# A two-layer flow-matching block: the latents' first stages written between the context's selection and its rows, and two raised priorities taken away

## The chip, the cores and the metric

The kernel runs on one core of one Trainium2 chip. The metric is the device time of one execution in microseconds (us), the median of several runs. Engines are named as in the profile: PE (matrix products, PEld its weight loads), DVE (vector engine), ACT (activations), POOL (GpSimd, which here also issues the indirect fetches), SP (issues the other transfers).

## What is computed

Two streams of 256 tokens of width 1024 go through two layers: the latents `x` and a context `z`. A layer is a mixer (a gated delta-rule scan in two directions, a pooling and a Fourier part, one output product) and a retrieval from 16384 experts, each with a residual. The latents' scan starts from the context's final scan state. The context is not updated in the second layer.

```python
def _peer(h, w_query, sub_keys, expert_u, expert_v):
    q = (h @ w_query).reshape(t, PEER_HEADS, 2, PEER_KEY_HALF)
    scores = jnp.einsum('thpc,hpnc->thpn', q, sub_keys)
    s_top, i_top = lax.top_k(scores, PEER_TOPK)            # 16 of 128, per head and half
    cand = s_top[:, :, 0, :, None] + s_top[:, :, 1, None, :]
    best, pos = lax.top_k(cand.reshape(t, PEER_HEADS, -1), PEER_TOPK)
    idx = ...                                              # 8 heads x 16 experts per token
    gate = jax.nn.softmax(best, axis=-1)
    act = gelu(einsum('td,thkd->thk', h, expert_u[idx]))
    return einsum('thk,thkd->td', gate * act, expert_v[idx])
```

## The kernel before

**Stages of layer 0 in the order of time.** The context's mixer runs first (`columns`, `scan`, `update`). Then two pieces of work are open side by side, and the change is about their order:

- The **context's retrieval**. `gather_select` scores the keys head by head (the products `po<-hT,w`, weights `in_wq` through one buffer per half, then `s<-keys,q` on L801) and picks the best on DVE (`select`, L772 to L884, with the multiply `oh` on POOL). Its last act is a transpose of the indices through PSUM bank `c2` (`c<-ident,idx_f`, L949, copied to `idx_t` on L950). Then `gather_rows` fetches one expert row per token and choice with indirect transfers from POOL (L970). For the first 128 tokens (`by_choice`) these are 128 fetches of `u` (512 KB each, seven buffers) with a dot product on DVE (L982) for each, and then 128 fetches of `v` with small products on PE (L1005) into PSUM bank `s`. For the other 128 tokens (`by_token`) there are 128 fetches of `uv`, 1 MB each. The loop `for _ in range(EARLY)` draws the first 256 fetches, all of `by_choice`, here; the rest is drawn in the middle of the stream below.
- The **latents' first stages**. `columns` makes the projections (`pj<-hT,w`, `pj<-w,hT`, the convolutions on L495 and L497) and the scan's gates (from L428 on, through the same single bank `c2`), `scan` makes the chunked scan (the multiplies `C<-L,levels`, `qd`, `kb`, `vb`, `kf` and the state's `S<-S,dc` run on POOL), `update` the output product and residual (L743 to L761), `dense_select` the latents' own selection, and `build` writes a table of gates (`gs`, L1089, L1090).

Then `stream` runs over all 128 blocks of experts for the latents (`first` L1118 to L1120, `second` L1141); its first product needs bank `s`, which `by_choice` holds until its last sum (L1010). The last 128 fetches run beside it, and after them the context's part of layer 1. Layer 1 then repeats mixer, selection and stream for the latents.

**What sets the order.** When the kernel is built, each engine gets one fixed list of instructions. The builder takes, among the instructions that are ready by its own estimate of time, the one with the highest priority. Priority is the place in the program, unless a block raises it: `tc.high_priority(AHEAD)` with `AHEAD = 100000` puts its block ahead of all that is written before it. Buffers and PSUM banks are given out in the order of the program. On the chip each engine works through its list in that order and stops where an operand is late.

Of the kernel before, what the change touches and what calls it, by code (L numbers as in the profile page):

```python
# [24 lines left out]
CTX, LAT = 0, 1  # L25
# [120 lines left out]
def _body(st, tc, a, out, dbg, until):  # L146
# [16 lines left out]
    def nm(s):  # L163
        n_names[0] += 1
        return f"{s}_{n_names[0]}"
# [46 lines left out]
    def dump(key, t):  # L212
        if dbg is not None and key in dbg:
            nc.sync.dma_start(dbg[key], t)
# [16 lines left out]
    def pool_tt(out, x, y, op):  # L231
        pool.tensor_tensor(out, x, y, op=op)  # L232
# [165 lines left out]
    def heads(tag, f):  # L398
        p = bank([128, 4, 128], tag)
        for h in range(4):  # L400
            f(p[:, h], h)
        return p
# [330 lines left out]
    def update(l, s, m, state, po, tl):  # L733
        zs, mix = state["zs"], state["mix"]
        parts = (("dmixh", F32R), ("dmixl", F32R)) if roles["split"] else (("dmix", F32),)
        dmix = [tl(name, [128, 4, T], 1, dt) for name, dt in parts]

        for b in range(NB):
            ot = tl(f"ot{b}", [128, 4, 128])
            ss = tl(f"ssq{b}", [128, 4])  # L740
            for h in range(4):
                act.activation(ot[:, h], po[b][:, h], AF.Square, accum_out=ss[:, h : h + 1])
            dve.tensor_scalar(ss, ss, 1.0 / 128, EPS, op0=OP.mult, op1=OP.add)  # L743
            r = rsqrt(ss, 4, f"c{b}")
            dve.tensor_tensor(ot, po[b], r[:, :, None].to_broadcast([128, 4, 128]), OP.mult)
            dve.tensor_tensor(ot, ot, zs[:, b].rearrange("p (h n) -> p h n", h=4), OP.mult)
            p = heads(f"c{b}", lambda o, h: pe.transpose(o, ot[:, h], ident))
            o = slice(b * 128, b * 128 + 128)
            if roles["split"]:
                act.copy(dmix[0][:, :, o], p)  # L750
                dve.tensor_tensor(dmix[1][:, :, o], p, dmix[0][:, :, o].bitcast(F32), OP.subtract)
            else:
                act.copy(dmix[0][:, :, o], p)
        dump(f"mixa{l}{s}", dmix[0])
        for n in range(2):
            g1 = in_rows(m[:, 2, :, s], n, "row1")
            cs = slice(n * 512, n * 512 + 512)
            for b, p in enumerate(columns_by_token(f"wout{l}", n, lambda k: [x[:, k % 4] for x in (dmix, mix)[k // 4]])):
                t = tl("upd", [128, 512], 2)
                dve.tensor_tensor(t, p, g1, OP.mult)  # L760
                dve.tensor_tensor(X[s, b][:, cs], X[s, b][:, cs], t, OP.add)  # L761
        for b in range(NB):
            dump(f"xm{l}{s}{b}", X[s, b])
# [278 lines left out]
    TG, IG = 16, 8  # L1042
    LAG = (17, 32)
    ROWS, EARLY = 7, 256
    AHEAD = 100000
    HB = {"u": 2, "v": 2}

    def dense_select(l, s, m, dp, side):

        Hh = dp("Hh", [128, KT, T], 1, F32R)  # L1050
        Hl = dp("Hl", [128, KT, T], 1, F32R)
        sp = Stage("select", side)
        chosen = dp("chosen", [128, 3, T])
        sc, sh = scales(l, 1, m, s)
        xns = [normed(X[s, b], sp("xn", [128, D], 2), f"n{b}") for b in range(NB)]
        hT = transposed(xns, sc, sh, sp("hT", [128, KT, T]))
        act.copy(Hh, hT)
        pool_tt(Hl, hT, Hh.bitcast(F32), op=OP.subtract)
        sel = sp("sel", [128, NB, 3, HEADS, TOPK])
        select(  # L1060
            l, sp, (Hh, Hl) if roles["split"] else (hT,), lambda h: sel[:, :, 0:2, h],
            lambda h, n: sel[:, :, 2, h : h + n], (HEADS,),
        )
        for b in range(NB):
            p = bank([128, 3, 128], f"c{b}")
            for i in range(3):
                pe.transpose(p[:, i], sel[:, b, i].rearrange("p h k -> p (h k)"), ident)
            act.copy(chosen[:, :, b * 128 : b * 128 + 128], p)
        sp.close()
        return Hh, Hl, chosen  # L1070

    def build(chosen, gdram, side, banks):

        bp = Stage("build", side)
        for tg in range(T // TG):
            gs = bp("gs", [128, NKEYS, TG], 2)
            for t4 in range(0, TG, 4):
                t0 = tg * TG + t4
                p = bank([128, 4, 128], banks[t0 // 4 % len(banks)])
                two = bp("two", [128, 4, 128], 3)  # L1080
                dve.tensor_tensor(  # L1081
                    two, chosen[:, 1, t0 : t0 + 4, None].to_broadcast([128, 4, 128]),
                    iota[:, None, :].to_broadcast([128, 4, 128]), OP.is_equal,
                )
                one = bp("one", [128, 4, 128], 3)
                for t in range(4):
                    key, gate = (chosen[:, i, t0 + t : t0 + t + 1] for i in (0, 2))
                    dve.tensor_scalar(one[:, t], iota, key, gate, op0=OP.is_equal, op1=OP.mult)  # L1088
                    pe.matmul(p[:, t], two[:, t], one[:, t], start=True, stop=True)  # L1089
                act.copy(gs[:, :, t4 : t4 + 4].rearrange("p i t -> p t i"), p)  # L1090
            nc.sync.dma_start(gdram[:, tg], gs)
        bp.close()
# [63 lines left out]
    def gdram():  # L1156
        return dr.tile([128, T // TG, NKEYS, TG], F32, tag="g", name=nm("gd"))


    m = mods[0]  # L1160
# [19 lines left out]
        chosen = gather_select(0, CTX, m, rows, lambda: (ck.close(), sw.close()))  # L1180
    cw.close()

    fetching = gather_rows(0, CTX, m, rows, chosen)
    for _ in range(EARLY):
        next(fetching)

    with tc.high_priority(AHEAD):
        lk, lc = Stage("keep", "right"), Stage("columns", "right")
        l_state = columns(0, LAT, m, True, lk, lc)
        lc.close()  # L1190
        ls = Stage("scan", "right")
        l_po = scan(0, LAT, True, l_state, ls)
        ls.close()
        lu = Stage("update", "right")
        update(0, LAT, m, l_state, l_po, lu)
        lu.close()
        lk.close()
    dp = Stage("dense", "right")
    su = Stage("stream_u", "right")
    with tc.high_priority(AHEAD):  # L1200
        Hh, Hl, keys = dense_select(0, LAT, m, dp, "right")
        gd = gdram()
        build(keys, gd, "right", ("c0", "c1"))
    sv = Stage("stream_v", "right")
    xdram = dr.tile([NB, 128, D], F32, tag="x", name="xd")
    for b in range(NB):
# [30 lines left out]
    m = mods[1]  # L1237
    sw, lk, lc = Stage("split", "right"), Stage("keep", "right"), Stage("columns", "right")
    with using(split=sw, lo="dve", c0="po", c1="po", c2="s", sb=1):
        l_state = columns(1, LAT, m, True, lk, lc)  # L1240
    lc.close()
    ls = Stage("scan", "right")
    l_po = scan(1, LAT, True, l_state, ls)
# [3 lines left out]
    lu = Stage("update", "right")  # L1247
# [5 lines left out]
    dp = Stage("dense", "right")  # L1253
    su = Stage("stream_u", "right")
    sw = Stage("split")
    with using(split=sw):
        Hh, Hl, keys = dense_select(1, LAT, m, dp, "right")
    sw.close()
    sv = Stage("stream_v")
    gd = gdram()  # L1260
# [32 lines left out]
```

## Time and profile before

| what | value |
|---|---|
| time, median of 3 runs | 3301.32 us (3293.26 to 3307.34) |
| the profiled execution's own time | 3294.41 us |
| its span | 3292.7 us |
| PE, PEld busy | 2858.5 us (87%), 2348.9 us (71%) |
| DVE busy | 2207.6 us (67%) |
| ACT, POOL busy | 1343.1 us (41%), 860.7 us (26%) |
| DMA | 746.52 MB, mean 227 GB/s |

The span runs from the first to the last instruction of the profiled execution. Busy time is the share in which an engine executed something. The stretch that the change touches lies between 296 us, where the context's mixer ends, and 1084 us, where the stream of layer 0 begins.

### The profile page before, as it was taken

What the parts mean: (1) busy time and instruction counts of PE and PEld (TensorE: products, weight loads), DVE (VectorE), ACT (ScalarE), POOL (GpSimd) and SP (SyncE); (2) the same over time, 40 slices, a digit from 0 to 9 for tenths busy, and PEclk for the clock granted to TensorE, in tenths of its full rate; (3) what the DMA queues carried; (4) which work ended last, traced back from release to release, by engine and by line L of the source; (5) the groups of instructions that cost most, each with busy time, mean ns of one, the idle gap of its engine ahead of it and who ended that gap; (6) DMA issues with size and microseconds to landing.
All of it is one profiled execution on the core that took longest, in us unless ns stands there. A gap on an engine that the chain in (4) does not pass through costs nothing. (4 is left out here: it accounts for less than half of the span.)

```text
span 3292.7 us, 47160 instructions
## 1 busy us (share of the span) xinstructions
PE 2858.5 (87%) x17467; PEld 2348.9 (71%) x17467; DVE 2207.6 (67%) x4920; ACT 1343.1 (41%) x2348; POOL 860.7 (26%) x638
## 2 busy tenths in 40 slices
PE   7998954778897888878789999999779889999998
PEld 4686744645452676767678999868578878889997
DVE  4534587789982688889895655652499955555555
ACT  4432212201251344444455645543335644544443
POOL 0140018985445333333310122134230000000000
PEclk8998976888899989999999999999889999999999
DMA  7622416589899999999985543361234575566663
GB/s 260 212 94 64 153 58 217 181 290 349 311 389 389 343 369 360 367 367 389 383 325 189 172 154 116 92 227 52 95 124 171 201 239 201 199 206 205 213 212 131
DMA packets 246165, 746.52 MB, mean 227 GB/s; under 512 B 21168, under 2 KB 94256, under 8 KB 225456
## 3 DMA queue, kind: packets, MB, share of 16 engines
q1 hardware_dynamic: 190320, 474.54, 41.8%
q0 software_dynamic: 55296, 268.46, 21.8%
q8 instruction: 137, 2.24, 0.3%
q14 instruction: 92, 0.75, 0.1%
q10 hardware_dynamic: 320, 0.52, 0.1%
HBM read 707.27 MB, written 35.65 MB: 226 GB/s over the span
## 5 line engine op out<-in xcount | busy, mean ns | idle before, releaser
L1118 PE MATMUL s<-Hh,hu 128*128 128x256 f32 x2048 | 601.5, 294 | 73.4 <-ACT hu L1107 50.5
L1120 PE MATMUL s<-Hh,lu 128*128 128x256 f32 x2048 | 599.5, 293 | 58.9 <-DVE lu L1108 58.9
L1119 PE MATMUL s<-Hl,hu 128*128 128x256 f32 x2048 | 592.2, 289 | 0.0
L1118 PEld LDWEIGHTS s<-Hh,hu 128*128 128x128 f32 x2048 | 404.7, 198 | 95.7 <-ACT hu L1107 58.2
L1108 DVE TENSOR_TENSOR lu<-w,hu 128x1024 fp32r<-128x1024 f32 x256 | 315.9, 1234 | 228.9 <-ACT hu L1107 228.8
L1120 PEld LDWEIGHTS s<-Hh,lu 128*128 128x128 f32 x2048 | 404.7, 198 | 72.1 <-DVE lu L1108 71.6
L1108 DVE TENSOR_TENSOR lv<-w,hv 128x1024 fp32r<-128x1024 f32 x256 | 314.9, 1230 | 173.3 <-ACT hv L1107 164.3
L1119 PEld LDWEIGHTS s<-Hl,hu 128*128 128x128 f32 x2048 | 405.0, 198 | 8.4
L1107 ACT CAST hu<-w 128x1024 fp32r<-128x1024 f32 x256 | 267.8, 1046 | 330.2 <-PE s L1119 253.0
L1107 ACT CAST hv<-w 128x1024 fp32r<-128x1024 f32 x256 | 267.4, 1044 | 159.8 <-PE pj L1141 116.1
L970 POOL DMA_INDIRECT uv<-in_uv,idx x128 | 206.9, 1616 | 405.1 <-DVE acc L1029 384.7
L982 DVE SCALAR_TENSOR_TENSOR uv<-uv,h 128x1024 f32<-128x1024 f32 x128 | 189.3, 1493 | 45.3 <-DMA uv<-in_u,idx 45.0
L232 POOL TENSOR_TENSOR C<-L,levels 128x512 f32<-128x512 f32 x96 | 137.8, 1446 | 290.4 <-DVE L L645 166.7
L970 POOL DMA_INDIRECT uv<-in_u,idx x128 | 177.6, 1387 | 45.3 <-issue 24.4
L1141 PE MATMUL po<-hv,wh 128*128 128x512 f32 x512 | 164.7, 402 | 14.3 <-ACT wh L1134 13.8
L970 POOL DMA_INDIRECT uv<-in_v,idx_t x128 | 131.1, 1024 | 129.1 <-PE s L1005 103.4
L1141 PE MATMUL po<-lv,wh 128*128 128x512 f32 x512 | 162.7, 399 | 0.1
L1141 PE MATMUL po<-hv,wl 128*128 128x512 f32 x512 | 162.2, 397 | 0.0
L1029 DVE SCALAR_TENSOR_TENSOR acc<-uv,dot,acc 128x1024 f32<-128x1024 f32 x127 | 162.2, 1277 | 0.0
L1141 PE MATMUL pj<-hv,wl 128*128 128x512 f32 x512 | 162.1, 397 | 0.0
L1141 PE MATMUL pj<-lv,wh 128*128 128x512 f32 x512 | 162.1, 396 | 0.0
L1141 PE MATMUL pj<-hv,wh 128*128 128x512 f32 x512 | 161.7, 397 | 0.0
(426 smaller groups left out, 5883.6 us busy)
## 6 DMA issues: line engine op xcount, KB each, us to landing
w<-in_tab SPq DMA_DIRECT2D x512, 512.0 KB, 4.6
w<-in_wmod SPq DMA_DIRECT2D x96, 512.0 KB, 4.7
gd<-gs SPq DMA_DIRECT2D x32, 1024.0 KB, 5.5
g<-gd SPq DMA_DIRECT2D x32, 1024.0 KB, 8.4
w<-in_wq SPq DMA_DIRECT2D x48, 512.0 KB, 4.0
w<-in_win SPq DMA_DIRECT2D x44, 512.0 KB, 4.2
w<-in_wrest SPq DMA_DIRECT2D x24, 512.0 KB, 3.7
w<-in_wout SPq DMA_DIRECT2D x24, 512.0 KB, 4.5
```

The lines of the kernel that those rows point to most:

```text
L232: pool.tensor_tensor(out, x, y, op=op)
L970: pool.indirect_dma_start(out=t, out_offset=None, in_=a[f"{table}{l}"], in_offset=bass.IndirectOffsetOnAxis(ap=index, axis=0))
L982: dve.scalar_tensor_tensor(u, u, 1.0, st["h2", b], op0=OP.mult, op1=OP.mult, accum_out=dots[:, j : j + 1])
L1029: dve.scalar_tensor_tensor(acc, uv[:, D:], dot, acc, op0=OP.mult, op1=OP.add)
L1107: act.copy(hi, raw)
L1108: eng(lo, raw, hi.bitcast(F32), op=OP.subtract)
L1118: pe.matmul(p, hi[:, ks], Hh[:, k], start=(k == 0), stop=False)
L1119: pe.matmul(p, hi[:, ks], Hl[:, k], start=False, stop=False)
L1120: pe.matmul(p, lo[:, ks], Hh[:, k], start=False, stop=(k == KT - 1))
L1141: pe.matmul(acc[b][n], x[:, ts], y[:, n * 512 : n * 512 + 512], start=(i == 0 and j == 0), stop=(i == NKEYS - 1 and j == 2),)
```

## The change

The call that makes the generator `fetching` and the loop that draws its first 256 fetches move down, behind the latents' `columns`, `scan`, `update`, `dense_select` and `build`. Both blocks `tc.high_priority(AHEAD)` go, and with them the constant. So priority now follows the program alone: the context's selection, then the latents' stages up to their gates, then the context's rows. Before, the latents' stages stood ahead of all else, and the selection and the rows followed. No instruction is added or taken away, and no size or buffer count changes.

```diff
-    AHEAD = 100000
...
         chosen = gather_select(0, CTX, m, rows, lambda: (ck.close(), sw.close()))
     cw.close()
 
+    lk, lc = Stage("keep", "right"), Stage("columns", "right")
+    l_state = columns(0, LAT, m, True, lk, lc)
+    lc.close()
+    ls = Stage("scan", "right")
+    l_po = scan(0, LAT, True, l_state, ls)
+    ls.close()
+    lu = Stage("update", "right")
+    update(0, LAT, m, l_state, l_po, lu)
+    lu.close()
+    lk.close()
+    dp = Stage("dense", "right")
+    su = Stage("stream_u", "right")
+    Hh, Hl, keys = dense_select(0, LAT, m, dp, "right")
+    gd = gdram()
+    build(keys, gd, "right", ("c0", "c1"))
     fetching = gather_rows(0, CTX, m, rows, chosen)
     for _ in range(EARLY):
         next(fetching)
 
-    with tc.high_priority(AHEAD):
-        lk, lc = Stage("keep", "right"), Stage("columns", "right")
...
-    dp = Stage("dense", "right")
-    su = Stage("stream_u", "right")
-    with tc.high_priority(AHEAD):
-        Hh, Hl, keys = dense_select(0, LAT, m, dp, "right")
-        gd = gdram()
-        build(keys, gd, "right", ("c0", "c1"))
     sv = Stage("stream_v", "right")
```

**PE, the end of the context's selection.** Before, the last heads' query products (`po`), their scores (`s`) and the indices' transpose (`c<-ident,idx_f`) follow each other, and the latents' gates (L428) come next:

```order
912 L256 MATMUL po_3117<-hT_2498,w_688_3115 128x256 x4
913 L801 MATMUL s_3138<-keys_3134,q_3136 128x128 x4
914 L256 MATMUL po_3215<-hT_2498,w_712_3211 128x256 x4
915 L256 MATMUL po_3215<-hT_2498,w_713_3213 128x256 x4
916 L256 MATMUL po_3215<-hT_2498,w_712_3211 128x256 x4
917 L256 MATMUL po_3215<-hT_2498,w_713_3213 128x256 x4
918 L801 MATMUL s_3236<-keys_3232,q_3234 128x128 x4
919 L949 MATMUL c_750_3355<-ident,idx_f_2527 128x128 x2
920 L428 MATMUL c_1032_4348<-hT_4281,wba_4346 16x256 x8
```

Now the latents' projections (`pj`) stand between the heads and between the last scores and the transpose:

```order
870 L256 MATMUL pj_829_3770<-hT_3369,w_3766 128x256 x2
871 L801 MATMUL s_3236<-keys_3232,q_3234 128x128 x4
872 L256 MATMUL pj_829_3770<-hT_3369,w_3766 128x256 x2
873 L256 MATMUL pj_829_3770<-hT_3369,w_3768 128x256 x4
...
889 L510 MATMUL c_831_3798<-ident,y_3788 128x128 x4
890 L527 MATMUL c_826_3760<-ident,fy_3739 128x128 x4
891 L949 MATMUL c_750_3355<-ident,idx_f_2527 128x128 x2
892 L256 MATMUL pj_846_3863<-w_3865,hT_3369 128x512 x2
...
896 L256 MATMUL pj_847_3864<-w_3867,hT_3369 128x512 x2
897 L428 MATMUL c_768_3436<-hT_3369,wba_3434 16x256 x8
898 L527 MATMUL c_836_3824<-ident,fy_3803 128x128 x4
```

What moved: the transpose is row 891 and no longer row 919; half of the second projection `pj<-w,hT`, the gates and the pooling and Fourier products now stand behind it.

**POOL, the end of the latents' scan.** Before, the fetches of `u` alternate with the scan's last state multiplies (`S`) like this; 76 of the 128 fetches stand ahead of the last multiply (row 194):

```order
184 L232 TENSOR_TENSOR S_5270<-S_1238_5224,dc_4400 128x512
185 L970 DMA uv_3574<-in_u,idx_2452 128x1024
186 L970 DMA uv_3577<-in_u,idx_2452 128x1024
187 L232 TENSOR_TENSOR S_5293<-S_1242_5247,dc_4400 128x512
...
192 L232 TENSOR_TENSOR S_1344_5648<-S_5270,dc_4400 128x512
193 L970 DMA uv_3592<-in_u,idx_2452 128x1024
194 L232 TENSOR_TENSOR S_1348_5671<-S_5293,dc_4400 128x512
```

Now 95 of the 128 stand ahead of it (row 213):

```order
205 L970 DMA uv_6940<-in_u,idx_2452 128x1024
206 L232 TENSOR_TENSOR S_4381<-S_978_4335,dc_3488 128x512
207 L970 DMA uv_6943<-in_u,idx_2452 128x1024
208 L970 DMA uv_6946<-in_u,idx_2452 128x1024
...
212 L970 DMA uv_6958<-in_u,idx_2452 128x1024
213 L232 TENSOR_TENSOR S_1084_4759<-S_4381,dc_3488 128x512
214 L970 DMA uv_6961<-in_u,idx_2452 128x1024
```

What moved: 19 fetches from behind the scan to ahead of its end. Ahead of the first state multiply stand 25 fetches and no longer 15.

**DVE, the start of the latents' selection.** Before, dots of the rows (L982) stand between the transposed inputs (L343) and the first pick (L772); 18 of the 128 stand behind the last residual of `update` (L761):

```order
984 L343 TENSOR_SCALAR hT_5903<-c_1404_5925,sc_5865,mod_80 128x256
985 L982 SCALAR_TENSOR_TENSOR uv_3721,dots_3366<-uv_3721,h_527_2457 128x1024
986 L982 SCALAR_TENSOR_TENSOR uv_3724,dots_3366<-uv_3724,h_527_2457 128x1024
...
992 L982 SCALAR_TENSOR_TENSOR uv_3742,dots_3366<-uv_3742,h_527_2457 128x1024
993 L772 MAX tv_5968<-sco_5966 128x8 x4
```

Now none does:

```order
1014 L343 TENSOR_SCALAR hT_4991<-c_1137_4992,sc_4953,mod_80 128x256
1015 L343 TENSOR_SCALAR hT_4991<-c_1138_4999,sc_4953,mod_80 128x256
1016 L343 TENSOR_SCALAR hT_4991<-c_1139_5006,sc_4953,mod_80 128x256
1017 L343 TENSOR_SCALAR hT_4991<-c_1140_5013,sc_4953,mod_80 128x256
1018 L772 MAX tv_5056<-sco_5054 128x8 x4
```

What moved: all 128 dots stand ahead of the latents' second norm. In the lists of PE, 17 of the 256 products of the `v` rows (L1005) now stand ahead of the latents' first head's scores; before, 13 stood ahead of the fifth head's, none ahead of the first's. Behind the last product of `build` (L1089, L1088 in the changed file) stand 95 of the 256 and no longer 103. In the lists of the stream and of layer 1 only neighbours change places.

## Rows read from the trace of the kernel before

**Rows 1.** Busy time by engine, granted PE clock and DMA, by stretch.
```profile
core 0: us, PE busy (x) PEld busy (x) DVE busy (x) ACT busy (x) POOL busy (x), PEclk, DMA share, GB/s
296.00:315.00 19.00, 16.75 (x80) 14.37 (x81) 8.92 (x36) 4.51 (x10) 0.00 (x0) 0.80 0.00 1
315.00:388.00 73.00, 73.00 (x300) 52.42 (x300) 30.23 (x100) 19.04 (x57) 2.38 (x1) 1.00 0.51 159
388.00:446.00 58.00, 54.46 (x283) 46.07 (x282) 38.93 (x255) 13.95 (x30) 3.82 (x2) 1.00 0.37 118
446.00:498.00 52.00, 12.14 (x59) 9.44 (x58) 50.91 (x273) 3.44 (x9) 11.81 (x7) 0.64 0.07 21
498.00:690.00 192.00, 129.31 (x801) 107.93 (x802) 152.93 (x213) 43.32 (x93) 174.09 (x124) 0.81 0.65 208
...
757.00:880.00 123.00, 99.16 (x493) 66.41 (x494) 117.19 (x573) 21.59 (x40) 67.29 (x53) 0.86 0.88 321
880.00:1010.00 130.00, 125.50 (x791) 72.89 (x789) 109.11 (x326) 70.39 (x75) 57.69 (x54) 0.99 0.99 380
1010.00:1084.00 74.00, 51.88 (x184) 6.90 (x183) 2.36 (x2) 0.58 (x1) 39.85 (x43) 0.91 0.97 363
1087.00:1705.00 618.00, 507.99 (x2920) 441.93 (x2920) 541.57 (x709) 270.93 (x583) 206.86 (x128) 0.93 0.98 370
```

**Rows 2.** Groups of DVE in 296 to 498: busy, mean ns, idle before.
```profile
L772 DVE MAX8 tv<-sco 128x8 f32<-128x128 f32 x32 | 7.4, 280 | 30.2 <-ACT sco L805 30.2
L495 DVE TENSOR_SCALAR y<-xpad,convw 128x256 f32<-128x256 f32 x12 | 3.7, 349 | 22.1 <-ACT xpad L491 22.1
```

**Rows 3.** Timeline of PE at the selection's end: start, us, instruction, idle before.
```profile
497.06 0.69 PE L949 MATMUL c<-ident,idx_f 128*128 128x128 f32 x2 [37.59 <-DVE idx_f L938]
498.26 5.20 PE L428 MATMUL c<-hT,wba 128*16 128x256 f32 x16 [0.52 <-DVE idx_t L950]
```

**Rows 4.** Groups of PE in 296 to 498.
```profile
L256 PE MATMUL po<-hT,w 128*128 128x256 f32 x256 | 60.1, 383 | 4.2 <-DMA w<-in_wq 4.2
...
L256 PE MATMUL pj<-w,hT 128*128 128x512 f32 x64 | 28.6, 592 | 0.0
```

**Rows 5.** Timeline of POOL, first fetch to the scan's last state multiply.
```profile
499.83 1.11 POOL L970 DMA_INDIRECT uv<-in_u,idx  x1 [0.16 <-issue]
...
521.93 2.20 POOL L232 TENSOR_TENSOR S<-S,dc 128x512 f32<-128x512 f32 x2
...
687.01 1.19 POOL L232 TENSOR_TENSOR S<-S,dc 128x512 f32<-128x512 f32 x1
```

**Rows 6.** The fetches of u among POOL's groups in 500 to 690.
```profile
L970 POOL DMA_INDIRECT uv<-in_u,idx x77 | 114.7, 1490 | 17.1 <-issue 13.8 <-DVE uv L982 0.6 <-PE pj L667 0.6
```

**Rows 7.** The dots among DVE's groups in 690 to 880.
```profile
L982 DVE SCALAR_TENSOR_TENSOR uv<-uv,h 128x1024 f32<-128x1024 f32 x54 | 69.3, 1302 | 12.8 <-DMA uv<-in_u,idx 12.6
```

**Rows 8.** Timeline: dots of DVE alone and beside a multiply of POOL.
```profile
536.64 1.22 DVE L982 SCALAR_TENSOR_TENSOR uv<-uv,h 128x1024 f32<-128x1024 f32 x1
...
538.39 2.71 DVE L982 SCALAR_TENSOR_TENSOR uv<-uv,h 128x1024 f32<-128x1024 f32 x1
...
538.73 1.29 POOL L232 TENSOR_TENSOR qd<-qd,qT 128x512 f32<-128x512 f32 x1
...
777.03 4.81 POOL L232 TENSOR_TENSOR Hl<-hT,Hh 128x2048 fp32r<-128x2048 f32 x1
...
777.27 5.65 DVE L982 SCALAR_TENSOR_TENSOR uv<-uv,h 128x1024 f32<-128x1024 f32 x1
```

**Rows 9.** Timeline of PE at the start of the stream.
```profile
1005.53 1.92 PE L1005 MATMUL s<-uv,wz 128*32 128x512 f32 x16
...
1082.19 1.06 PE L1005 MATMUL s<-uv,wz 128*32 128x512 f32 x6 [0.21 <-DMA uv<-in_v,idx_t]
1083.94 0.38 PE L1118 MATMUL s<-Hh,hu 128*128 128x256 f32 x1 [0.70 <-ACT sum L1010]
```

**Rows 10.** Longest waits of PE's loads in 1010 to 1084: total, times, longest.
```profile
PEld s L1005 <- DMA uv<-in_v,idx_t: 66.1, 45, 4.8
```

More of the change, by code (lines that the diff above doesn't have):

```diff
@@ L1185, in _body @@
         next(fetching)
-    with tc.high_priority(AHEAD):
-        lk, lc = Stage("keep", "right"), Stage("columns", "right")
[L1189 to L1197, printed above, removed]
-    dp = Stage("dense", "right")
-    su = Stage("stream_u", "right")
-    with tc.high_priority(AHEAD):
-        Hh, Hl, keys = dense_select(0, LAT, m, dp, "right")
-        gd = gdram()
-        build(keys, gd, "right", ("c0", "c1"))
     sv = Stage("stream_v", "right")
```

## The prediction

> **What bounds the kernel now.** I read first the table of busy time by stretch [rows 1], to see which engine is full where. Up to 388 us PE is full (73.0 of 73 us) and DVE is not (30.2); from 446 to 498 it is the other way round: DVE 50.9 of 52 us, PE 12.1, POOL 11.8, DMA 7%. So 296 to 498 us is one stretch of work in which two engines take turns: the latents' projections go first and fill PE, the context's selection comes late and fills DVE. The groups of DVE say what DVE missed meanwhile: it waited 30.2 us for scores and 22.1 us for projections to convolve [rows 2]. The timeline of PE shows what ends the stretch: the transpose of the indices at 497.06 after 37.6 us of idle time, released by the selection's last index, and right behind it the latents' gates, which use the same bank [rows 3]. So at about 497.8 us, which I call T0, both the fetches of rows and the latents' scan get free.
>
> Next the timeline of POOL [rows 5]: the first fetch at 499.83, the last state multiply of the scan at 687.01. POOL is busy 174 of 192 us there [rows 1]; fetches and the scan's multiplies share it, so POOL paces this part. From 757 to 880 DVE is full (117.2 of 123 us). From 880 on the DMA is (0.97 to 0.99). The timeline of PE shows the end: the stream's first product at 1083.94 waits for the last sum of the `v` products [rows 9], and those wait for their rows 66.1 us in the last 74 [rows 10]. Behind that the stream runs with DMA at 0.98 for 618 us. It will take as long wherever it begins, so what the start of the stream gains, the end of the kernel gains.
>
> **The change, part by part.** It moves; nothing is added.
>
> *T0.* Selection and projections now interleave on PE and DVE, so the two full stretches can lie side by side. Bounds: PE was busy 16.75 + 73.0 + 54.5 + 12.1 = 156.4 us from 296 to 498 [rows 1]. Behind the transpose stand now half of the second projection, 28.6 / 2 = 14.3 us [rows 4], and smaller products. That leaves at most 142 us: T0 at 438 if PE never waits. DVE was busy 8.9 + 30.2 + 38.9 + 50.9 = 129 us, which gives 425, and some 12 us more because no scores exist before the first head's. Both engines have about the same work, and each waits for the other: PE on weights of the next head (one buffer for each half; 4.2 us of such waits before [rows 4]), DVE on the last head's chain. I add 10 us to the floor of PE: **T0 at 448, 50 us earlier**. The other end: as much waiting stays as DVE shows now, 30.2 + 22.1 = 52 us [rows 2], so 438 + 52 = 490, a gain of 8.
>
> *The scan.* Here the new order costs. Behind T0 stand now also the second half of a projection, and 95 instead of 76 fetches come ahead of the last state multiply. A fetch takes POOL (114.7 + 17.1) / 77 = 1.71 us with the idle time before it [rows 6]. 19 more take 32.5 us. Before, the last multiply started 687.0 − 497.8 = 189 us behind T0; now about 222, at 670. I take the whole price, since POOL had 18 us idle in 192 and most of that belongs to the fetches. The other ends: 20 us if the fetches fit partly into idle time, 48.5 with the lock below.
>
> *Update and the latents' selection.* 18 dots that stood behind the last residual are gone from there. A dot takes 1.30 us [rows 7]: 23.4 us. One of them was the dot of 5.65 us that stood beside the long multiply `Hl`, 4.4 us over the usual 1.22 [rows 8]; `Hl` now comes behind all dots. Together 27.8 us on an engine that is full there; I take 24, since some of the small norm operations will wait where dots stood, and keep 12 and 28 as ends.
>
> *The new wait.* 17 products of the `v` rows now stand on PE ahead of the latents' first head's scores. They need nine rows, and with seven buffers the last two can only be fetched when the first are used up. Behind them on PE wait the scores, and for those DVE. The trace shows no such place; a wait for a `v` row was at most 4.8 us [rows 10]. Nothing to 10 us (two rows); I take 5.
>
> *The tail.* Behind `build` stand 95 products instead of 103, four rows fewer. 103 took from 1005.5 to 1083.2 [rows 9], 1.5 us a row: 6 us less.
>
> *Sum at the start of the stream:* −50 + 32.5 − 24 + 5 − 6 = −42.5 us, so 1041 and not 1084. The profiled execution took 3294.4 us, 3252 then; the median of the runs shown is 6.9 us above it (3301.3), so I forecast **3259 us** for the median.
>
> **A rule beside the rows.** The dot that ran beside POOL's multiply took 2.71 us and the one just before 1.22 [rows 8]: 1.49 us more, about the 1.29 us of the multiply. So the two seem to exclude each other, and the new order puts 19 more fetches, and with them up to 19 more dots, beside the scan's multiplies. If 11 of them, the growth between the first `qd` and the last state multiply, each met one, the scan would lose 11 × 1.49 = 16 us more. I leave it out of the sum, since the count of multiplies does not grow and dots already stand beside all of them. The Trainium skill speaks against the change here ("SBUF — State Buffer", section Who interferes with whom): a DVE instruction with two SBUF inputs contends with a GpSimd instruction that reads SBUF, under an exclusive lock. By that rule the trace agrees, and a sum in which every added dot met a multiply would be −26.5.
>
> **The rivals.**
> - *More than that.* The scan is not stretched: POOL's added fetches fit where it waited, the price is 20 us and not 32.5, the new wait is nothing and T0 nears its floor: −60 + 20 − 24 − 6 = −70, 3231 us. For it speaks that POOL's idle time in front of fetches is 17.1 us [rows 6]; against it that PE and DVE would have to run without a gap.
> - *The gain is paid back.* The order was made with estimated times. If the interleaved selection stops often (PE waits for a convolution that stands on DVE behind a pick, DVE for scores behind a projection), T0 is about 480: −18 + 32.5 − 24 + 5 − 6 = −10.5, 3291 us. For it speaks that each list is fixed and the two depend on each other in both directions.
> - *Slower.* The pacing on POOL. With the lock at every added dot the scan costs 48.5 us, and it decides once T0 gains less than some 20 us and only 12 us of the dots come back: −15 + 48.5 − 12 + 5 − 6 = +20, 3322 us. For it speaks that POOL is the fullest engine there; against it that T0 has to lose most of what [rows 2] show as free.
> - *No effect.* The stream waits for the last `v` row, so an earlier T0 would not help if that row came at the same time. But from 446 to 498 DMA moved 21 GB/s and POOL was idle [rows 1], and this hole closes; I give it no chance of its own.
>
> **How the numbers follow.** The forecast with T0 between 438 and 465, −60 to −25: 0.56. More than that: 0.14. Paid back: 0.20, of which I count a quarter as still faster by over 0.5% (16.5 us, about what a measurement of this kernel can tell from no change). Slower: 0.10, a third of it within 0.5%. So faster 0.56 + 0.14 + 0.05 = 0.75, same 0.15 + 0.03 = 0.18, slower 0.07. The range reaches on the low side to the first rival's 3231, on the high side past the second's 3291 to no change: 3230 to 3302. The likeliest case alone is 3240 to 3277.
>
> **What would show it.** Right: the transpose L949 near 448 with little idle time ahead of it, PE and DVE both over 85% busy from 315 to there; the last state multiply some 222 us behind; no dot behind the latents' last residual; the stream's first product at 1030 to 1060, and the distance from there to the end as before within some 5 us. Wrong: L949 behind 470 with waits for `y` or for scores; a distance from T0 to the last state multiply of 240 or of 190; the scores of the latents' first head waiting for `uv`; or a stream that itself gets longer or shorter by more than the start moved.

## The result, and the profile after

| | before | after |
|---|---|---|
| median time, 13 runs each | 3301.32 us (3291.72 to 3310.16) | 3276.61 us (3257.59 to 3285.62) |
| ratio after/before | | 0.9926 (95%: 0.9907 to 0.9945) |
| the profiled execution's own time, its span | 3294.41, 3292.7 us | 3268.07, 3266.3 us |

The changed kernel is 0.74% faster, 24.7 us by the medians. Forecast was 3259, a gain of 42.3 us on that median. Of the missing 17.6 us some 9 are missing where the stream starts, and some 7 lie behind it, where, as shown below, executions with one and the same order differ by more than that; the rest is the distance of the profiled execution from the median.

Busy time by stretch of the changed kernel, answering to [rows 1] (sum of busy time and count per engine, granted PE clock, DMA share):

```profile
core 0: us, PE busy (x) PEld busy (x) DVE busy (x) ACT busy (x) POOL busy (x), PEclk, DMA share, GB/s
296.00:441.00 145.00, 131.90 (x630) 109.27 (x631) 122.34 (x661) 39.87 (x93) 17.58 (x9) 0.96 0.38 116
441.00:511.00 70.00, 54.19 (x220) 36.63 (x218) 54.11 (x98) 22.75 (x65) 48.69 (x42) 0.77 0.80 284
511.00:665.00 154.00, 108.86 (x632) 88.93 (x632) 128.33 (x161) 28.04 (x48) 139.83 (x100) 0.77 0.66 206
665.00:757.00 92.00, 68.35 (x255) 37.41 (x255) 65.19 (x148) 12.73 (x32) 64.88 (x49) 0.84 0.91 338
757.00:851.00 94.00, 78.08 (x425) 53.12 (x423) 85.95 (x508) 14.15 (x30) 36.56 (x31) 0.95 0.77 263
851.00:1010.00 159.00, 142.18 (x847) 75.25 (x846) 110.53 (x326) 69.97 (x73) 76.93 (x72) 0.98 0.99 375
```

The first row is the point of the change: from 296 us to the end of the context's selection PE is busy 132 of 145 us and DVE 122. Before, the two took turns, and the selection ended 202 us behind 296 and not 145 [rows 1].

The timeline of PE (start, us, instruction, idle time before it and what ended it) at the selection's end answers to [rows 3]:

```profile
424.56 9.18 PE L256 MATMUL pj<-w,hT 128*128 128x512 f32 x21
...
439.12 1.12 PE L527 MATMUL c<-ident,fy 128*128 128x128 f32 x4 [4.95 <-DVE fy L521]
440.63 0.69 PE L949 MATMUL c<-ident,idx_f 128*128 128x128 f32 x2 [0.39 <-DVE idx_f L938]
441.11 10.73 PE L256 MATMUL pj<-w,hT 128*128 128x512 f32 x20
451.77 3.63 PE L428 MATMUL c<-hT,wba 128*16 128x256 f32 x16
...
484.84 1.13 PE L601 MATMUL c<-fy,fw 128*128 128x256 f32 x4 [0.73 <-ACT fy L598]
```

The transpose L949 stands at 440.63 and not at 497.06, with 0.39 us of idle time ahead of it where there were 37.59. But behind it PE still has 45 us of the latents' stages to do (39.6 of them busy): the rest of a projection, the gates, and the pooling and Fourier products up to L601.

POOL's timeline answers to [rows 5]:

```profile
443.40 1.11 POOL L970 DMA_INDIRECT uv<-in_u,idx  x1 [0.16 <-issue]
...
487.13 2.04 POOL L232 TENSOR_TENSOR S<-S,dc 128x512 f32<-128x512 f32 x2
...
665.51 1.25 POOL L232 TENSOR_TENSOR S<-S,dc 128x512 f32<-128x512 f32 x1
```

The last state multiply starts 224.9 us behind L949; before it was 190.0. And the start of the stream, which answers to [rows 9]:

```profile
1048.86 1.06 PE L1005 MATMUL s<-uv,wz 128*32 128x512 f32 x6 [0.17 <-DMA uv<-in_v,idx_t]
1050.61 0.39 PE L1117 MATMUL s<-Hh,hu 128*128 128x256 f32 x1 [0.69 <-ACT sum L1010]
```

So the stream starts 33.3 us earlier, still right behind the last `v` row. From there to the end of the span it is 2215.7 us, against 2208.8 before.

### The profile page after: what moved, and what is told of

It reads as the page before. It is cut to its first block, busy times and chain, and to the rows that moved or that the text cites. A ratio compares the mean times of both kernels' runs of the same rounds, so it can differ in the third digit from the quotient of the medians.

```text
span 3266.3 us, 47152 instructions
## 1 busy us (share of the span) xinstructions
PE 2874.7 (88%) x17467; PEld 2362.5 (72%) x17467; DVE 2211.1 (68%) x4920; ACT 1349.3 (41%) x2352; POOL 860.3 (26%) x638
## 5 line engine op out<-in xcount | busy, mean ns | idle before, releaser
L1106 ACT CAST hu<-w 128x1024 fp32r<-128x1024 f32 x256 | 267.8, 1046 | 328.3 <-PE s L1118 252.6
L982 DVE SCALAR_TENSOR_TENSOR uv<-uv,h 128x1024 f32<-128x1024 f32 x128 | 193.4, 1528 | 38.7 <-DMA uv<-in_u,idx 37.8
L1133 ACT CAST wh<-we 128x256 fp32r<-128x256 f32 x256 | 103.4, 404 | 143.0 <-DVE we L1132 78.3
L1088 PEld LDWEIGHTS c<-one,two 128*128 128x128 f32 x1024 | 123.6, 193 | 53.3 <-issue 33.2
```

Source lines behind the costliest of these rows:

```text
L982: dve.scalar_tensor_tensor(u, u, 1.0, st["h2", b], op0=OP.mult, op1=OP.mult, accum_out=dots[:, j : j + 1])
L1106: act.copy(hi, raw)
L1133: act.copy(wh, w)
```

## The experiments

Each kernel was profiled once and timed beside the kernel before. The table puts the profiled executions side by side, in us: T0 is here the start of L949's last product, "scan" the distance from there to the last sum of a state (`Sn` on DVE, L716), then the first fetch of `v`, the first product of `build` (L1088), the stream's first product, and the time from there to the end of the span. The last column is the ratio of the timed runs to before, with its 95% interval.

| kernel | T0 | scan | first v | build | stream | to the end | ratio |
|---|---|---|---|---|---|---|---|
| before | 497.3 | 191.9 | 786.3 | 882.3 | 1083.9 | 2208.8 | |
| columns raised (e1) | 500.7 | 189.0 | 786.1 | 882.0 | 1083.4 | 2218.6 | 0.9987 (0.9972 to 1.0002) |
| short dots in before (e4) | 501.2 | 190.6 | 784.1 | 884.1 | 1084.7 | 2218.8 | 1.0015 (1.0002 to 1.0028) |
| after | 440.9 | 233.6 | 722.8 | 851.5 | 1050.6 | 2215.7 | 0.9926 (0.9907 to 0.9945) |
| after again (a2) | 440.3 | 234.6 | 726.4 | 857.9 | 1054.9 | 2217.9 | 0.9914 (0.9890 to 0.9938) |
| gates in c1 (e2) | 442.7 | 231.7 | 732.9 | 866.4 | 1066.1 | 2211.6 | 0.9879 (0.9859 to 0.9899) |
| gates in c1 again (e12) | 444.7 | 219.9 | 720.9 | 854.5 | 1052.9 | 2209.8 | 0.9924 (0.9894 to 0.9955) |
| multiplies on ACT (e3) | 438.9 | 218.0 | 714.5 | 844.3 | 1042.8 | 2222.8 | 0.9881 (0.9862 to 0.9900) |
| both (e5) | 447.3 | 208.8 | 713.4 | 847.9 | 1051.4 | 2211.5 | 0.9848 (0.9827 to 0.9869) |
| scan raised (e7) | 441.6 | 205.3 | 717.4 | 834.5 | 1044.1 | 2220.2 | 0.9873 (0.9852 to 0.9893) |
| all three (e8) | 447.1 | 212.6 | 710.8 | 842.5 | 1040.2 | 2219.4 | 0.9869 (0.9848 to 0.9891) |
| v raised (e9) | 439.2 | 237.0 | 730.4 | 880.7 | 1046.1 | 2215.7 | 0.9895 (0.9876 to 0.9915) |
| e5 and v raised (e10) | 445.3 | 211.3 | 716.3 | 866.8 | 1033.1 | 2227.9 | 0.9851 (0.9828 to 0.9873) |
| e8 and v raised (e11) | 443.2 | 212.5 | 710.8 | 863.2 | 1028.2 | 2222.5 | 0.9857 (0.9834 to 0.9881) |

**e1, is it the place of `columns` alone?** The kernel after, with one block raised again:

```diff
-    l_state = columns(0, LAT, m, True, lk, lc)
+    with tc.high_priority(100000):
+        l_state = columns(0, LAT, m, True, lk, lc)
```

> After, with the latents' columns alone raised ahead of everything again. Theory: the whole change is the place of columns against the selection, so this is the kernel before: indices' transpose L949 within 3 us of 497, last state multiply within 5 of 687, stream from 1084 within 5, time within 0.4% of before (3301). Rival: drawing the rows behind the latents' stages, or the scan to build without a raised priority, gives a part: the stream starts at 1075 or earlier, 3290 or less. It also shows how much the stretch from the stream's start to the end of the span (2209 before, 2216 after) differs between profiled executions: by 5 us or more if the 7 us are chance, by under 2 if they are not.

With this one block raised, the fixed lists of all five engines are those of before, row for row but for the numbers of the buffers. The time is that of before too. So drawing the rows further down, and not raising `scan`, `update`, `dense_select` and `build`, does nothing that can be told from chance. The change is that the context's selection is no longer kept behind the latents' projections. As a second execution of one and the same program it also shows what chance does: T0 3.4 us later (a little more than the 3 expected), and 2218.6 instead of 2208.8 us from the stream's start to the end.

**a2, after once more.**

> After, unchanged, for a second profiled execution. In the first the stream starts 33 us earlier than before, while the medians differ by 25. If the difference is chance of the execution (its own time was 8.5 us under the median), this one has its places elsewhere: T0 within 3 us of 441, the stream's start between 1050 and 1062, and the stretch from there to the end anywhere from 2209 to 2223, as the other profiled executions show. If the stream is really longer with this change, that stretch is 2216 again and the start within 2 us of 1051.

T0 and the scan are the same within 1 us; from the last residual on, 3 to 6 us came later. The stretch behind the stream's start is 2217.9 us. With before at 2208.8 and 2218.6, the 6.9 us that the first pair of profiles shows there are no cost of the change. The gain at the stream's start is 29 to 33 us, the medians differ by 24.7 and 29.3.

**e4, the dots behind the residual.** The kernel before with

```diff
+                n = D if j < 110 else 8
                 dve.scalar_tensor_tensor(
-                    u, u, 1.0, st["h2", b], op0=OP.mult, op1=OP.mult, accum_out=dots[:, j : j + 1]
+                    u[:, 0:n], u[:, 0:n], 1.0, st["h2", b][:, 0:n], op0=OP.mult, op1=OP.mult,
+                    accum_out=dots[:, j : j + 1]
                 )
```

> Before, with the last 18 of the 128 dots of by_choice (those that stand on DVE behind the latents' last residual) cut to 8 of 1024 columns, so the context's dots of those choices are not the reference's. All fetches stay. It takes some 20 us off DVE just where the change took dots away. The prediction's step: DVE is full there, so the latents' first pick and build's start come 18 to 24 us earlier (build at 860, stream at 1062, 3280). Rival: PE needs the time for the norm's transposes and the first head's query products anyway, and the dots stood beside that; the first pick comes 2 to 6 us earlier (now 29 us behind the last residual), build's start 3 to 8, stream 1076 to 1082, 3295.

This kernel leaves out most of what those 18 dots add up. Nothing is gained in the end: build at 884.1 and not 882.3, the time 0.15% above before. DVE got the time and waits with it. The timelines of DVE and of PE of this kernel, up to the latents' first pick:

```profile
776.18 4.06 DVE L983 SCALAR_TENSOR_TENSOR uv<-uv,h 128x8 f32<-128x8 f32 x1 [1.10 <-DMA uv<-in_u,idx]
...
785.19 0.87 DVE L772 MAX8 tv<-sco 128x8 f32<-128x128 f32 x4 [4.77 <-ACT q L797]
```

```profile
747.85 7.03 PE L256 MATMUL pj<-w,mix 128*128 128x512 f32 x16
763.89 0.66 PE L337 MATMUL c<-ident,xn 128*128 128x128 f32 x2 [9.02 <-DVE uv L983]
...
772.26 11.39 PE L256 MATMUL pj<-hT,w 128*128 128x256 f32 x52
783.49 2.00 PE L801 MATMUL c<-keys,q 128*128 128x128 f32 x16
```

The first pick needs the first head's scores (L801), and those need the last residual, the norm, the transposes of L337 and 64 query products. That chain takes from 763.89 to 785 on PE. Before, the dots ran beside it: the first scores were copied out by 786.1, and the pick began at 787.4, when the last of these dots ended. Behind the last residual the first pick comes after 26.0 us; in before and e1 it took 30.1 and 29.9. So 17 short dots behind that residual (in the trace the first of the 18 stands just ahead of it) are worth 4 us and not 18 to 24. The step of the prediction is refuted, and the rival holds up to the pick (2 to 6 us). Its numbers for build, stream and time missed: the 4 us are gone again at build. What lost them is not shown; behind the first pick the trace has the rows of PE and POOL in another order than before, so this kernel tests the way to the first pick alone.

**e3, the pace of the scan.** In the latents' layer-0 scan `vb`, `kb`, `kf` and `S` go to ACT; the kernel is after otherwise:

```diff
+        def mul(out, x, f, n=4):
+            if (l, s) != (0, LAT):
+                return pool_tt(out, x, f[:, :, None].to_broadcast([128, 4, 128]), op=OP.mult)
+            for h in range(4):
+                act.activation(out[:, h], x[:, h], AF.Copy, scale=f[:, h : h + 1])
...
-            pool_tt(vb, vtok[:, b], fac[:, 0, b, dsl, None].to_broadcast([128, 4, 128]), op=OP.mult)
+            mul(vb, vtok[:, b], fac[:, 0, b, dsl])
```

> After, with the 18 multiplies vb, kb, kf and S of the latents' layer-0 scan on ACT (four instructions with a factor per head each) and no longer on POOL, where they take 4.3 + 4.5 + 4.2 + 7.8 = 20.8 us between T0 and the last state multiply. Theory: POOL's list (fetches and multiplies) paces the scan; the last sum of a state (L716 on DVE) comes 15 to 25 us earlier than in after, and the stream too by 10 to 20: 3260. Rival: the scan's chain through PE, DVE and ACT paces it and POOL's work fits in; under 6 us, stream within 5 us of 1051, 3277.

The last sum of a state, by DVE's timeline, in after and in e3:

```profile
674.46 0.69 DVE L716 TENSOR_TENSOR S<-S,c 128x512 f32<-128x512 f32 x1 [1.72 <-PE c L710]
```

```profile
656.88 0.69 DVE L722 TENSOR_TENSOR S<-S,c 128x512 f32<-128x512 f32 x1 [2.93 <-PE c L716]
```

It comes 17.6 us earlier for 20.8 us of POOL, the stream 7.8 us earlier than in after (12.1 than in a2). POOL's work paces the scan, as the theory has it; half of the gain is gone by the time the stream starts. It is lost between the last sum and the first pick, by the two rows below (after, then e3; columns as in [rows 1]):

```profile
674.46:763.65 89.19, 65.54 (x249) 35.28 (x252) 57.56 (x136) 13.90 (x34) 57.96 (x45) 0.87 0.91 338
656.88:753.59 96.71, 73.32 (x249) 37.77 (x252) 60.59 (x142) 13.72 (x34) 58.21 (x46) 0.82 0.88 321
```

For the same number of products PE was busy 7.8 us longer in e3, at a granted clock of 0.82 and not 0.87, and the stretch is 7.5 us longer. a2, the kernel of after again, had 0.81 there and took 93.2 us. So some of this loss may be the execution's and not the edit's.

Part of the gain in the scan came through DVE. Its groups over the scan, for after (486 to 666) and e3 (484 to 657):

```profile
L982 DVE SCALAR_TENSOR_TENSOR uv<-uv,h 128x1024 f32<-128x1024 f32 x73 | 126.9, 1757 | 23.0 <-DMA uv<-in_u,idx 22.6
```

```profile
L988 DVE SCALAR_TENSOR_TENSOR uv<-uv,h 128x1024 f32<-128x1024 f32 x73 | 109.0, 1511 | 22.5 <-DMA uv<-in_u,idx 22.4
```

73 dots in both, but 17.9 us less for them: 18 multiplies of POOL fewer, and so about 1 us each. Whether the scan got shorter through POOL's own list or through these dots, which share DVE with it, e3 does not separate.

**e2 and e12, the start of the scan.** After, with `bank(..., "c2")` of the latents' layer-0 gates (L426, L431, L454, L473) turned into `bank(..., "c1")`.

> After, with the four small PSUM tiles of the latents' gates in bank c1 and no longer in c2, so that the gates need not wait for the indices' transpose (T0, 441 in after). Theory 1: of the 35 us that the scan lost against T0, 22 lie ahead of its first state multiply, since the gates start only behind T0; with the gates done before it the first state multiply comes 10 to 20 us nearer to T0 (46 in after, 24 in before), the last one too, and the stream starts 10 us earlier (1041), time 3267. Theory 2: not the gates but the rest of the projections, the pooling and the Fourier products on PE (done at T0+45) hold the scan's start: the first state multiply stays at T0+40 to 46, stream within 4 us of 1051. Theory 3: POOL's fetches set the scan's end whatever its start: first state multiply earlier, the last one still T0+220 to 226.

> The gates in bank c1 once more, for a second profiled execution, since the first was 16 us above the median of its kernel and showed the gain neither in T0 nor in the scan. If the gates' earlier start is the cause, the scan's first masked product again comes at T0+39 and an execution near the median has the last state multiply at 655 to 662 and the stream's start at 1036 to 1045. If the gain is in T0 or behind the stream's start, it shows there: T0 at 430 or less, or under 2205 us from the stream's start to the end.

The gates now stand at 324 to 329 us, long before T0. The scan's first masked product (`L` on DVE) comes at T0+39 in both executions, 45 in after: 6 us. The first state multiply stands at T0+39 to 40 and not 46, short of the 10 to 20 us of theory 1, so theory 2 comes nearest for the start; what holds it is seen below, at e7. The last state multiply stands at T0+222.6 in the first execution, as theory 3 has it, and at T0+214.3 in the second. The time remains open. The first timing gave 0.9879, the second 0.9924, the same as after; the two scans differ by 12 us from one execution to the other, and the stream of the second starts at 1052.9, as in after and not at 1036 to 1045. I can't show a gain of this edit alone.

**e5, both.**

> After, with both edits: the gates in bank c1 and the 18 multiplies on ACT. Alone they took 13.5 and 10.6 us off the median of after. Theory 1, two separate places (start of the scan and POOL's list): the gains add, 3252. Theory 2, both shorten the same stretch and the next limit (the norm's and first head's products, then DMA) takes the rest: 3259 to 3264.

0.9848: close to the sum of both in the first timings, but the profiled execution shows a stream at 1051.4, T0 6 us later than in after, and a `v` part of 338 us. The time is better than that of after (the intervals do not touch); where the second part of it comes from is not shown.

**e7 and e8, the scan ahead of all else.** Besides the gates in `c1`, the pooling and Fourier products use bank `po` and no longer `c0` and `c1`, and `scan` is raised:

```diff
+    with tc.high_priority(100000):
+        l_po = scan(0, LAT, True, l_state, ls)
```

> After with the gates in bank c1, and besides the latents' scan raised ahead of everything and the pooling and Fourier products in bank po, so that they no longer hold c0 and c1 ahead of the scan. Theory: the rest of PE's work behind T0 holds the scan's start; the first masked product (L on DVE) comes at T0+28 to 33 instead of 39 with the gates alone and 45 in after, the last sum of a state as much earlier, 3254 to 3258. Rival: the scan's end is set by POOL's list, and an earlier start is given back: last sum within 4 us of T0+232, time 3263 like the gates alone.

> All three: gates in c1, scan raised with pooling and Fourier products in po, the 18 multiplies on ACT. If start and pace of the scan are two separate costs: first masked product at T0+28 to 33, last sum of a state at T0+200 to 208 (218 with the multiplies on ACT alone), time 3243 to 3250. If one hides the other: last sum at T0+212 or later, 3258 or more.

The first masked product comes at T0+44 (e7) and T0+47 (e8), no earlier than in after: the theory on the start is refuted. What holds it can be read from the last Fourier product on PE and the first masked product on DVE. In e7 (for after, L601 stands at 484.84 for 1.13 us, as shown above):

```profile
484.57 1.13 PE L603 MATMUL po<-fy,fw 128*128 128x256 f32 x4 [0.73 <-ACT fy L600]
```

```profile
485.89 0.69 DVE L634 TENSOR_TENSOR L<-c,mask_l 128x512 f32<-128x512 f32 x1 [0.94 <-issue]
```

And the same row of DVE in after:

```profile
486.16 0.69 DVE L632 TENSOR_TENSOR L<-c,mask_l 128x512 f32<-128x512 f32 x1 [1.10 <-issue]
```

In after and in e7, as in eight of the nine other kernels and executions with the new order, the scan's first masked product starts 0.19 us behind the end of the last Fourier product, whatever the bank and the priority (0.54 in e11); before, the Fourier products were done 98 us ahead of it. A likely reason is that the scan's buffers take the place of those of `columns`, which the program closes just ahead of the scan and which the Fourier products read last. A higher priority for the scan can't change that. No run moved these buffers, so the reason is argued and not shown.

Yet the scan of e7 is 28 us shorter than in after (15 to 26 than with the gates in `c1` alone). Its list on POOL has 86 fetches ahead of the last state multiply where after has 95; nine at 1.71 us [rows 6] would be 15 us of it. The time is that of the rival, 3263.8 us, though the rival had the scan's end wrong too. `build` starts 17 us earlier, and the stream only 6.5. With the multiplies on ACT besides (e8) the scan is no shorter: the last sum at T0+212.6 and 3261.0 us are what was expected if one hides the other.

So from the first fetch of `v` to the stream it takes about as long, whatever ends earlier on the latents' side: 327.8 us in after, 328.3 in e3, 326.7 in e7. In before and e1 it took 297.6 and 297.3.

Where the gain of e7 went is seen by splitting the time from `build` to the stream at the last product of `build`. `build` itself takes 120 to 127 us in all these kernels. Behind its last product the list of PE still holds products of `v` rows, and the time from there to the stream follows their number:

| kernel | products behind `build` | us from there to the stream |
|---|---|---|
| v raised (e9) | 51 | 39.7 |
| after, a2 | 95 | 72.2, 72.2 |
| before, e1 | 103 | 78.6, 78.8 |
| both (e5) | 111 | 83.6 |
| scan raised (e7) | 115 | 86.9 |

That is 0.75 to 0.78 us a product, some 1.5 us a row, in every one. In e7 ten rows more than in after stand behind `build`, and these take back 14.7 of the 17 us (`build` itself is 4.2 us shorter there). That led to the last question, whether the rows can be used up earlier.

**e9 to e11, the rows of `v` first.** After, and e5 and e8, with

```diff
-    for _ in range(EARLY):
-        next(fetching)
+    for _ in range(EARLY // 2):
+        next(fetching)
+    with tc.high_priority(100000):
+        for _ in range(EARLY // 2):
+            next(fetching)
```

> After, with the 128 v rows (their fetches and the products that use them up) raised ahead of the latents' stages. On PE 52 rows' products then stand ahead of build's first product, where after has 30 and before 28. Theory: in after the v rows wait for products that stand on PE behind the latents' query products while the DMA is at 0.77 (757 to 851 us) and the stretch from the first v fetch to the last is 320 us against 289 in before; used up earlier, the rows fill that hole (94 x 0.23 = 22 us of DMA), build starts later by 8 to 15 us, and the stream starts 10 to 20 us earlier: 1032 to 1042, 3257 to 3267. Rival: from build on the DMA is full with the table's writes whatever stands ahead, and build is then the last to end; what build starts later, the stream starts later: 1055 to 1065, 3280 to 3290.

> The same on top of the gates in bank c1 and the 18 multiplies on ACT (3255 without it). By the theory the hole in the DMA is filled here too: stream at 1025 to 1040, 3235 to 3247. By the rival 3258 to 3270.

> The same on top of all three edits (gates in c1, scan raised with pooling and Fourier in po, multiplies on ACT; 3261 without it). There the latents' selection ended early and the gain of 9 to 17 us at build's start was given back up to the stream. By the theory the rows were what was late: stream 10 to 20 us earlier, 3241 to 3251. By the rival 3262 or more.

Busy time of e9 by stretch, from the latents' selection on:

```profile
757.00:870.00 113.00, 110.02 (x496) 59.12 (x498) 78.82 (x482) 15.35 (x28) 56.03 (x48) 0.99 0.82 280
870.00:1010.00 140.00, 131.32 (x829) 73.89 (x822) 114.53 (x351) 71.47 (x77) 64.02 (x59) 0.99 1.00 390
1010.00:1045.00 35.00, 22.36 (x88) 3.04 (x86) 2.36 (x2) 0.00 (x0) 16.47 (x18) 1.00 1.05 387
```

PE is full now where DMA was at 0.77, DMA goes up to 0.82 only, and `build` starts 23 to 29 us later, not 8 to 15. Still the part from the first `v` to the stream falls from 328 to 315.7 us, and the stream starts 4.5 to 9 us earlier than in the two executions of after: with 51 products left behind `build` and not 95, 32.5 us are saved there for 23 to 29 us of a later `build`. The time is 0.9895, some 10 us under after, with intervals that overlap. So the mechanism is there in the places, about half as large as expected, and not clear of chance in the time; the rival, that all is given back and more, is refuted. e10 and e11 show the same on top of the others (316.8 and 317.4 us instead of 338 and 329.4) and have the earliest streams of all. Their medians are the lowest, 3250.8 and 3250.4 us: for e10 between what theory and rival had, for e11 at the slow end of the theory. By the ratios they are no better than e5, and e11 no better than e8. All three are faster than both kernels of the case, at about 0.985 of before. In e3, e10 and e11 the stretch from the stream's start to the end is 2222 to 2228 us, longer than in before or after; whether something is given back there or it is chance, these runs don't tell.

## Why the prediction was right, and where its sum was off

The sign and the place were right: the stream starts earlier because T0 does, part of it is paid back in the scan, and nothing behind the stream changes. The sum at the stream's start was −42.5 and is −33.3 (−29 in a2). Term by term, by the first profiled executions (after against before) and by the second (a2 against e1, whose lists are those of before):

| step | forecast | measured | by a2 and e1 |
|---|---|---|---|
| T0 | −50 | −56.4 (497.06 to 440.63) | −60.4 |
| scan, T0 to last state multiply | +32.5 | +34.9 (189.95 to 224.88) | +39.3 |
| from there to the first pick: dots −24, new wait +5 | −19 | −2.3 (100.4 to 98.1) | +2.0 |
| first pick to the first product of build | none | −7.0 (94.8 to 87.8) | −5.0 |
| build, first to last product | none | +3.9 (123.1 to 126.9) | +2.3 |
| tail, behind build's last product | −6 | −6.4 (78.6 to 72.2) | −6.6 |
| sum | −42.5 | −33.3 | −28.5 |

*T0: right, and 6 us better than forecast.* PE and DVE lie side by side: from 315 us to L949 PE is busy 92% of the time and DVE 90%. The 10 us added for waits were about right, since PE stood idle for 13 us from 296 on. What was too high was its floor: PE worked 132 us ahead of L949 and not 142. More than half a projection had moved behind the transpose, and the granted clock was 0.96 in this stretch, where before it was 0.64 from 446 on [rows 1]; how the 10 us split between these two is not shown.

*The scan: nearly the right price, in part by luck, for a reason of which only a part holds.* I charged all 32.5 us to 19 more fetches on POOL. But 22.8 of the 34.9 us pass ahead of the scan's first masked product (T0+22.5 before, T0+45.3 after), while PE ends the projection and the pooling and Fourier products; the first masked product starts 0.19 us behind their end. POOL is not full there: 28.7 of 45 us, and ten of the 19 fetches stand in that time. The other 12.1 us lie between the first masked product and the last state multiply, where nine more fetches stand; those at 1.71 us are 15. That POOL's work paces this part is shown by e3, though not whether through its list or through the dots. Counted to the last sum, as in the table of experiments, the scan costs 41.7 us, and the way to the first pick gains 9.0 (45.6 and 4.3 by a2 and e1).

*The step that failed is "Update and the latents' selection".* "18 dots that stood behind the last residual are gone from there ... on an engine that is full there" counted DVE's busy time as its path. Measured, the first pick comes 100.4 us behind the last state multiply before and 98.1 after; in e1 and a2 it is 102.7 and 104.7. Behind the last residual it is 30.1 and 29.9 us before, 26.5 and 27.7 after. So the 24 us came to 2 to 4 where the dots went. (17 of the 18 stand behind that residual in the trace, and two of these behind the first pick.) What took their place is a wait of DVE for the first scores; the longest waits of DVE in after, 665 to 860:

```profile
DVE tv L772 <- ACT sco L805: 14.6, 1, 14.6
DVE uv L982 <- DMA uv<-in_u,idx: 8.7, 11, 1.7
```

It is not the wait that I had priced. PE waits for no `v` row ahead of those scores; it is busy with the norm's transposes and the query products, which the dots had covered. e4 shows it from the other side: with the dots cut short, before gains 4 us up to the first pick and nothing in the time. The wait for a `v` row exists too, once and behind the picks, in PE's timeline:

```profile
827.61 3.19 PE L1005 MATMUL s<-uv,wz 128*32 128x512 f32 x8 [7.02 <-DMA uv<-in_v,idx_t]
```

From the first pick to build 5 to 7 us were gained for which the sum had nothing: before and e1 give 94.8 and 94.8, after and a2 87.8 and 89.8. The two executions with the gates in `c1` give 92.3 and 94.6, so this may be chance in part. Two dots of 1.2 us that stood behind the first pick before are gone from there; the rest of the cause is not shown.

*The tail: right.* Behind `build`'s last product it shrank by 6.4 us, four rows at 1.5 us, as forecast. Ahead of it `build` itself took 2.3 to 3.9 us longer, for which the sum had nothing; there DMA is at 0.98 to 0.99. The two stretches, first to last product of `build` and from there to the stream, in before and then in after:

```profile
882.30:1005.30 123.00, 119.26 (x757) 71.61 (x754) 107.51 (x322) 68.51 (x72) 54.38 (x50) 0.99 0.99 380
1005.30:1083.90 78.60, 55.76 (x209) 7.66 (x207) 2.36 (x2) 1.60 (x2) 42.37 (x45) 0.91 0.97 366
```

```profile
851.50:978.40 126.90, 120.42 (x761) 72.07 (x760) 107.66 (x322) 68.58 (x72) 57.79 (x52) 0.99 0.98 371
978.40:1050.60 72.20, 49.31 (x193) 6.92 (x192) 2.36 (x2) 1.98 (x3) 38.39 (x41) 0.98 0.99 377
```

*Seen along the fetches* the same gain reads: the first fetch 56 us earlier, the part of `u` 7 us shorter, the part of `v` 30 us longer. The forecast had no term of this kind. e9 shows a part of why it is longer: the products that use up the `v` rows stand on PE behind the latents' query products, and raised ahead of them they give back 12 of the 30 us. The rest is not shown.

*The rule beside the rows.* I left out the 16 us by which added dots could meet POOL's multiplies. The mean dot in the scan went from 1702 ns (63 dots, 106.6 us, before, 520 to 687) to 1757 (73 dots). Above the 1.22 us of a dot alone that is 30 us before and 39 after: 9 us more. The Trainium skill ("SBUF — State Buffer", Summary: rules for kernel authors) says that of such two instructions the second one to issue blocks until the first ends. The short dot of e4, which began 0.5 us behind the multiply and ended with it, agrees. The order of the two does not always decide here: in the scan of after 32 dots took over 1.35 us, each beside a multiply, and in 15 of these cases the dot's row begins first and it is still the dot that takes longer, as in the first pair of [rows 8].

## What to carry to other kernels

Busy time taken off a full engine is a gain only if what stands next does not wait for another engine: before counting it, follow the first instruction behind the removed ones back to its operands, and see how long those need by themselves. When two long pieces of work are allowed to interleave, ask at the join what the one still has to do: here 45 us on PE behind T0, which the old order had done ahead of it. And follow the transfers as well as the latents' chain: this stream waits for the last row, and every row left behind `build` cost it 1.5 us, however early `build` came.

## What the runs showed of the hardware that was not expected

A dot over 8 columns takes 0.15 us, but 4.06 us beside POOL's `Hl` (775.67 to 780.22): it ends when POOL's multiply ends. Before, the full dot took 5.65 us at the same place [rows 8]. So the cost here is that of POOL's instruction and not of the dot's size. The timeline of POOL in e4:

```profile
775.67 4.55 POOL L232 TENSOR_TENSOR Hl<-hT,Hh 128x2048 fp32r<-128x2048 f32 x1 [1.37 <-issue]
```

And one program's executions differ in where the clock of PE falls. From the scan's last sum to the latents' first pick the two executions of after ran at granted clocks of 0.87 and 0.81 and took 89 and 93 us; the two executions with the gates in `c1` (e2, e12) had 0.76 and 0.86 there and took 100 and 95. With changes of a few us, one profile shows places, and only several show prices.
